# 1 / rms per column by a transpose on VectorE and two transfers of GpSimd's queue; squares and mean in one pass

## The chip, the core and the metric

The kernel runs on one core of a Trainium2 chip. The metric is the time of one execution in device microseconds; three executions of the kernel before took 994.14, 994.19 and 994.27 us, median 994.19. The engines are named as the profile names them: PE (TensorE; PEld is its weight load), DVE (VectorE), ACT (ScalarE), POOL (GpSimd) and SP (SyncE, which here only issues transfers).

## The reference

Two layers of a streaming encoder on 256 tokens of width 1024. Each layer has a half-step SwiGLU feed-forward part, a token mixer (latent attention with rotary keys in layer 0, forgetting attention in layer 1), a second half-step feed-forward part, and a gated embedding added to the residual; one norm ends the trunk. Each of these parts reads a normed residual:

```
def rms_norm(x, g):
    y = x * lax.rsqrt(jnp.mean(x * x, axis=-1, keepdims=True) + NORM_EPS)
    return y * g

def swiglu(x, w_in, w_out):
    gate, up = jnp.split(x @ w_in, 2, axis=-1)
    return (jax.nn.silu(gate) * up) @ w_out

for i in range(2):
    h = h + 0.5 * swiglu(rms_norm(h, ffn_norm[i, 0]), ffn_w_in[i, 0], ffn_w_out[i, 0])
    u = rms_norm(h, mix_norm[i])
    h = h + (mla_mixer if i == 0 else fox_mixer)(u, ...)
    h = h + 0.5 * swiglu(rms_norm(h, ffn_norm[i, 1]), ffn_w_in[i, 1], ffn_w_out[i, 1])
    h = h + jax.nn.sigmoid(rms_norm(h, ple_norm[i]) @ ple_w_gate[i]) * (p[i] @ ple_w_proj[i])
return rms_norm(h, final_norm)
```

## The kernel before

**Data.** The residual lies transposed as `hT`: 128 partitions by 8 blocks of the width, 256 tokens as columns. Activations and weights are f32, each split into a high part and the rest (`u`, `whi`, `wlo`), and a product is the sum of three products of the parts. A weight arrives as a 128x1024 tile `raw` (SP issues the transfer, four buffers); ACT copies its high part (`high`, L101), DVE subtracts it (`low`, L105), and seven pairs of parts can be alive. `W.pump()` adds one such step to the streams of ACT, DVE and SP; `W.get()` takes the next weight for PE.

**Order.** Nothing is reordered: each engine runs its instructions in the order in which the code adds them, and waits where an operand is not there yet.

**The norm.** `Norm` multiplies the residual by the gain and leaves 1 / rms for later: it is a factor of each token, so it can be applied to the product. While the residual's blocks come out, ACT squares them and POOL adds the squares up (`acc`, L303). `by_token` (L312) sums over partitions on PE (`pst`, L317), DVE makes the mean (`v`, L320) and POOL takes it to the power -1/2 (`rtok`, L322: 128 tokens on partitions, two columns). `by_column` (L324) turns that into a row of 256 columns on all partitions: PE multiplies `rtok`, repeated 128 times, by the identity (`pb`, L327), and ACT copies the product to `rb` (L330).

**The feed-forward part** (`ffn`, L334). The gate and up products of row block c go to two banks `pg` and `pu`; there are seven banks for all such products. The first pair (c = 0) is made by `blocks`, whose last steps wait for the residual's last blocks, then c = 1, and so on up to 21. `evacuate` multiplies a bank by `rb` on DVE (`two`, L341), POOL adds the two halves (`gu`, L343), ACT takes silu (`sg`), POOL multiplies (`hid`), and ACT and DVE split the product (`hs`). No bank is evacuated before `rb` is there. In the code before, `by_token` stands behind the gate block of c = 1 and `by_column` behind its up block.

**The other users.** `fox` uses `rb` in `project`, after its value products; there `by_token` comes at (c, k) = (0, 5) and `by_column` at (1, 0). `mla` and `ple` use it too. `by_column` stands in eight places of the run: the four feed-forward parts, twice in `mla`, once in `ple`, once in `fox`.

**The end** (`ple_by_token`, L865) works with tokens on partitions. `gated` applies the sigmoid, multiplies and adds to `h`, and lets ACT square `h` with a running sum (L885); `weigh` multiplies by the last gain (L888), `mean` adds a sum to the mean on DVE (L893), `root` takes the power on POOL (L906), `store` scales and sends the rows out. This runs over five pieces: 512 columns for each half of the tokens, then 512, 256 and 256.

Of the kernel before, what the change touches and what calls it, by code (L numbers as in the profile page):

```python
# [144 lines left out]
def trunk(ctx, tc, xT, xt, pT, pos, freq, bf, lead0, lead1, ffn_in, ffn_out, w_down, w_uq, w_ukv, mla_o,  # L145
# [7 lines left out]
    psum = ctx.enter_context(tc.tile_pool(name="psum", bufs=7, space=bass.MemoryType.PSUM))  # L153
    psm = ctx.enter_context(tc.tile_pool(name="psm", bufs=1, space=bass.MemoryType.PSUM))
# [55 lines left out]
    nc.gpsimd.memset(ones, 1.0)  # L210
    mhalf = const.tile([P, 2], F32, name="mhalf")
# [61 lines left out]
    class Norm:  # L273
# [38 lines left out]
        def by_token(self):  # L312
# [8 lines left out]
            self.rtok = work.tile([P, 2], F32, name="rtok", bufs=3)  # L321
            nc.gpsimd.tensor_tensor(self.rtok, v, mhalf, op=ALU.pow)  # L322

        def by_column(self):  # L324
            pb = psm.tile([P, T], F32, name="pb", tag="small")
            for t in range(2):
                nc.tensor.matmul(pb[:, t * P:(t + 1) * P], self.rtok[:, t:t + 1].to_broadcast([P, P]), ident,  # L327
                                 start=True, stop=True)
            self.rb = work.tile([P, T], F32, name="rb", bufs=3)
            nc.scalar.activation(self.rb, pb, AF.Copy)  # L330
            self.rb2 = self.rb.rearrange("p (o t) -> p o t", o=1).to_broadcast([P, 2, T])


    def ffn(norm, nxt, then=None, first=None, meanwhile=None, later=None):  # L334
# [38 lines left out]
        else:  # L373
            blocks(waits[0], norm.pair)
            W.pump(2)
        at = len(waits)
        for c in range(at, KF):
            pg = bank("pg")
            block(pg, norm.pair)
            if c == at:  # L380
                if not first:
# [6 lines left out]
            if c == at:  # L388
                norm.by_column()
# [309 lines left out]
    def fox(norm, nxt):  # L699
# [50 lines left out]
        for c in range(3):  # L750
            pv = [bank("pv0", (P, FV)), bank("pv1", (P, FV))]
            for k in range(KD):
# [6 lines left out]
                if (c, k) == (0, 5):  # L759
                    norm.by_token()  # L760
                elif (c, k) == (1, 0):
                    norm.by_column()
# [103 lines left out]
    def ple_by_token(pp, norm):  # L866
# [6 lines left out]
        sums = work.tile([P, 2, 3], F32, name="sums", bufs=1)  # L873
# [5 lines left out]
        def gated(t, ps, a, i):  # L879
# [5 lines left out]
            nc.scalar.activation(sg, h[:, t, a], AF.Square, accum_out=sums[:, t, i:i + 1])  # L885
# [3 lines left out]

        def mean(t, i):  # L890

            v = work.tile([P, 1], F32, name="v1", bufs=4)
            nc.vector.tensor_scalar(v, sums[:, t, i:i + 1], 1.0 / D, means[t], op0=ALU.mult, op1=ALU.add)  # L893
            means[t] = v
# [47 lines left out]
        for t in range(2):  # L942
            gated(t, ps[t], half[0], 0)
            weigh(t, half[0])
            mean(t, 0)
# [9 lines left out]
        gated(0, lasts[0], cuts[0], 1)  # L955
        weigh(0, cuts[0])
        mean(0, 1)
        root(0)
        gated(1, lasts[1], cuts[1], 1)
        store(0, [(nc.vector, a) for a in half])  # L960
        weigh(1, cuts[1])
        mean(1, 1)
        gated(1, lasts[2], cuts[2], 2)
        weigh(1, cuts[2])
        mean(1, 2)
# [176 lines left out]
    for i in range(2):  # L1142
# [98 lines left out]
```

## Time and profile before

| | |
|---|---|
| median of 3 executions | 994.19 us |
| the profiled execution | 994.27 us |
| its span, first to last instruction | 992.5 us |
| outside the span | 1.8 us |
| PE busy | 983.4 us, 99% of the span |
| DVE busy | 741.5 us, 75% |
| ACT busy | 515.3 us, 52% |
| POOL busy | 423.4 us, 43% |
| granted clock of PE, mean | 0.998 |

Busy time is that of an engine's instructions; overlapping ones are counted once. Matmuls are pipelined, so the time that one costs PE is the distance between the starts of its neighbours, not its own duration. An engine's idle time is put down to the event that ended it.

### The profile page before, as it was taken

The page shows a single profiled execution, that of the slowest core. Times are in us where ns is not written, and L with a number is a line of the kernel's source. Part 1 is how long each engine was busy: PE and PEld are TensorE (multiplying, and loading weights), DVE is VectorE, ACT ScalarE, POOL GpSimd, SP SyncE. Part 2 cuts the span into 40 slices and gives each one's busy share as a digit, 9 for nine tenths or more (in the row PEclk, how much of TensorE's full clock was granted, in tenths as well). Part 3 has the DMA queues.
Part 4 walks back from the last instruction along what each step waited for, and adds up shares of the span by engine and source line. Part 5 has one row for each costly group of instructions (what it writes and reads, how often), then busy time and mean ns, then how long its engine had stood idle before and what let it go on. Part 6 is the DMA issues. An engine that isn't in the chain of part 4 may idle for free.

```text
span 992.5 us, 15922 instructions
## 1 busy us (share of the span) xinstructions
PE 983.4 (99%) x5850; PEld 869.4 (88%) x5850; DVE 741.5 (75%) x1089; ACT 515.3 (52%) x820; POOL 423.4 (43%) x348
## 2 busy tenths in 40 slices
PE   9999999999999999999999999999999999999996
PEld 7888888998988888889988888899889888888885
DVE  6777879686878877667878786666877778786674
ACT  7555444466555544446655444446455555444552
POOL 0777730110277675111477773120211577761110
PEclk9999999999999999999999999999999999999999
DMA  8576666563456666665466666656543576666561
GB/s 324 184 249 209 198 180 192 175 194 105 148 172 207 182 188 175 205 203 168 149 210 203 186 184 180 193 179 217 149 149 106 177 209 196 187 179 204 179 210 43
DMA packets 53406, 182.26 MB, mean 184 GB/s; under 512 B 6225, under 2 KB 7761, under 8 KB 53201
## 3 DMA queue, kind: packets, MB, share of 16 engines
q1 hardware_dynamic: 52752, 180.40, 58.8%
q8 instruction: 46, 0.75, 0.3%
q10 hardware_dynamic: 576, 0.85, 0.3%
q14 instruction: 32, 0.25, 0.1%
HBM read 179.00 MB, written 1.05 MB: 181 GB/s over the span
## 4 chain that ended last, share of the span: by engine, by line
PE 98%; DMA 1%; issue 0%; ACT 0%; DVE 0%; SPq 0%; POOLq 0%; POOL 0%
PE po L247 16%; PE pu L247 16%; PE pg L247 16%; PE po L248 8%; PE pg L248 8%; PE pu L248 8%; PE ps L247 5%; PE ps L248 2%; PE ps L232 2%; PE ps L234 2%; PE ps L233 2%; PE pv L232 1%; PE pv L234 1%; PE pv L233 1%; PE po L476 1%; PE psc L794 1%
## 5 line engine op out<-in xcount | busy, mean ns | idle before, releaser
L105 DVE TENSOR_TENSOR wlo<-raw,whi 128x1024 fp32r<-128x1024 f32 (+2 forms) x339 | 417.0, 1239 | 13.2 <-ACT whi L101 12.6
L101 ACT ACTIVATE whi<-raw 128x1024 fp32r<-128x1024 f32 (+2 forms) x339 | 335.3, 1022 | 25.3 <-DMA raw<-in_ffn_in_dram 11.1
L343 POOL TENSOR_TENSOR gu<-two 128x256 f32<-128x256 f32 x176 | 234.7, 1334 | 122.5 <-DVE two L341 113.1
L247 PE MATMUL pg<-u,whi 128*128 128x512 f32 x702 | 251.1, 395 | 0.0
L247 PE MATMUL pu<-u,whi 128*128 128x512 f32 x702 | 250.9, 395 | 0.0
L247 PE MATMUL po<-hs,whi 128*128 128x512 f32 x704 | 246.8, 394 | 0.0
L248 PE MATMUL po<-hs,wlo 128*128 128x256 f32 x704 | 197.2, 280 | 0.0
L248 PE MATMUL pg<-u,wlo 128*128 128x256 f32 x702 | 197.0, 281 | 0.2 <-DVE wlo L228 0.2
L248 PE MATMUL pu<-u,wlo 128*128 128x256 f32 x702 | 196.8, 280 | 0.0
L247 PEld LDWEIGHTS po<-hs,whi 128*128 128x128 f32 x704 | 132.1, 188 | 31.3
L247 PEld LDWEIGHTS pg<-u,whi 128*128 128x128 f32 x702 | 131.8, 188 | 31.1 <-ACT whi L997 0.3
L247 PEld LDWEIGHTS pu<-u,whi 128*128 128x128 f32 x702 | 131.8, 188 | 30.9
L248 PEld LDWEIGHTS pg<-u,wlo 128*128 128x128 f32 x702 | 132.1, 188 | 0.7 <-DVE wlo L228 0.7
L248 PEld LDWEIGHTS po<-hs,wlo 128*128 128x128 f32 x704 | 132.3, 188 | 0.0
L248 PEld LDWEIGHTS pu<-u,wlo 128*128 128x128 f32 x702 | 132.0, 188 | 0.0
L303 POOL TENSOR_TENSOR acc<-acc,sq 128x256 f32<-128x256 f32 x42 | 46.2, 1101 | 174.2 <-ACT sq L298 152.7
L224 ACT ACTIVATE hs<-hid 128x256 fp32r<-128x256 f32 x88 | 36.8, 418 | 144.6 <-POOL hid L361 142.4
L361 POOL TENSOR_TENSOR hid<-sg,gu 128x256 f32<-128x256 f32 x88 | 106.3, 1208 | 6.9
L228 DVE TENSOR_TENSOR hs<-hid,hs 128x256 fp32r<-128x256 f32 x88 | 63.0, 716 | 49.7 <-ACT hs L224 49.7
L341 DVE TENSOR_TENSOR two<-pg,rb 128x512 f32<-128x512 f32 x88 | 60.3, 686 | 46.1 <-PE pg L248 38.6
L287 ACT ACTIVATE u<-state 128x256 fp32r<-128x256 f32 x47 | 24.0, 511 | 122.5 <-DVE state L408 104.3
L355 ACT ACTIVATE sg<-gu 128x256 f32<-128x256 f32 x88 | 36.8, 418 | 77.9 <-POOL gu L343 77.9
(258 smaller groups left out, 1162.2 us busy)
## 6 DMA issues: line engine op xcount, KB each, us to landing
raw<-in_ffn_in_dram SPq DMA_DIRECT2D x172, 512.0 KB, 4.0
raw<-in_ffn_out_dram SPq DMA_DIRECT2D x64, 512.0 KB, 3.6
raw<-in_ffn_out_dram SPq DMA_DIRECT2D x32, 384.0 KB, 3.4
raw<-in_fox_qk_dram SPq DMA_DIRECT2D x16, 512.0 KB, 4.5
raw<-in_mla_o_dram SPq DMA_DIRECT2D x8, 512.0 KB, 5.3
raw<-in_ple_gate_dram SPq DMA_DIRECT2D x8, 512.0 KB, 5.2
raw<-in_fox_o_dram SPq DMA_DIRECT2D x8, 512.0 KB, 3.5
raw<-in_ple_rows_dram SPq DMA_DIRECT2D x8, 512.0 KB, 4.6
```

What stands on the lines that cost most here:

```text
L101: self.nc.scalar.activation(self.pairs[i][0][:, c], self.raws[i][:, c], AF.Copy)
L105: self.nc.vector.tensor_sub(lo[:, c], self.raws[i][:, c], hi[:, c].bitcast(F32))
L224: nc.scalar.activation(hi, src, AF.Copy)
L228: nc.vector.tensor_sub(lo, src, hi.bitcast(F32))
L232: nc.tensor.matmul(ps, w[0], x[0], start=first, stop=False)
L247: nc.tensor.matmul(ps, hi, x[:, k], start=k == 0, stop=False)
L248: nc.tensor.matmul(ps[:, 1, :], lo, x[:, k, 0, :], start=False, stop=k == last)
L303: nc.gpsimd.tensor_add(new, self.acc, sq)
L341: nc.vector.tensor_mul(two, ps, norm.rb2)
L343: nc.gpsimd.tensor_add(gu[c, i], two[:, 0, :], two[:, 1, :])
L355: nc.scalar.activation(sg, gu.pop((c, 0)), AF.Silu)
L361: nc.gpsimd.tensor_mul(hid[c], gu.pop((c, 0)), gu.pop((c, 1)))
```

## The change

Three parts, told by what they do.

1. `spread` takes the place of `by_column` in three of the eight places: the second feed-forward part of layer 0, `fox`, and the second feed-forward part of layer 1. `by_token(soon=True)` writes `rtok` into columns 0 and 32 of a 128x64 tile `wide` that is zero elsewhere. DVE transposes `wide` in blocks of 32x32 (`turned`), so that the 256 factors lie in rows of 32 on four partitions. A transfer of POOL's queue writes them to a row of 256 in DRAM, and a second one reads that row back onto all 128 partitions, as `rb`. The other five places keep `by_column` (the first feed-forward part of layer 1 by `soon=False`).
2. In those two feed-forward parts `by_token` and `spread` stand ahead of the blocks of c = 1: one `W.pump()`, `by_token`, one `W.pump()`, `spread`. In `fox`, `by_token` stays at (0, 5) and `spread` stands at (0, 7).
3. In `ple_by_token` the squares and their mean are made by one DVE instruction (`tensor_tensor_reduce`, which starts its sum from the mean so far) instead of ACT's square and `mean`.

```diff
@@
+    dram = ctx.enter_context(tc.tile_pool(name="dram", bufs=1, space=bass.MemoryType.DRAM))
@@
+    wide = const.tile([P, 2 * 32], F32, name="wide")
+    nc.gpsimd.memset(wide, 0.0)
+    firsts = wide.rearrange("p (t j) -> p t j", t=2)[:, :, 0]
@@
-        def by_token(self):
+        def by_token(self, soon=False):
...
-            self.rtok = work.tile([P, 2], F32, name="rtok", bufs=3)
+            self.rtok = firsts if soon else work.tile([P, 2], F32, name="rtok", bufs=3)
             nc.gpsimd.tensor_tensor(self.rtok, v, mhalf, op=ALU.pow)
@@
+        def spread(self):
+
+            turned = work.tile([P, 2 * 32], F32, name="turned", bufs=1)
+            nc.vector.transpose(turned, wide)
+            row = dram.tile([1, T], F32, name="row", bufs=4)
+            nc.gpsimd.dma_start(row.rearrange("o (t q j) -> (o q) t j", t=2, q=4),
+                                turned.rearrange("(q r) (t j) -> q r t j", q=4, t=2)[:, 0])
+            self.rb = work.tile([P, T], F32, name="rb", bufs=3)
+            nc.gpsimd.dma_start(self.rb, row.to_broadcast([P, T]))
+            self.both()
@@
             blocks(waits[0], norm.pair)
-            W.pump(2)
+            W.pump()
+            if soon:
+                norm.by_token(soon=True)
+            W.pump()
+            if soon:
+                norm.spread()
@@
             if c == at:
-                if not first:
+                if not (first or soon):
                     norm.by_token()
                 W.pump()
@@
             if c == at:
-                norm.by_column()
+                if first or not soon:
+                    norm.by_column()
@@
                 if (c, k) == (0, 5):
-                    norm.by_token()
-                elif (c, k) == (1, 0):
-                    norm.by_column()
+                    norm.by_token(soon=True)
+                elif (c, k) == (0, 7):
+                    norm.spread()
@@
             nc.vector.tensor_add(h[:, t, a], h[:, t, a], sg)
-            nc.scalar.activation(sg, h[:, t, a], AF.Square, accum_out=sums[:, t, i:i + 1])
+
+            v = work.tile([P, 1], F32, name="v1", bufs=4)
+            nc.vector.tensor_tensor_reduce(sg, h[:, t, a], h[:, t, a], 1.0 / D, means[t], op0=ALU.mult, op1=ALU.add,
+                                           accum_out=v)
+            means[t] = v
@@
-            ffn(n0, n1, AF.Exp)
+            ffn(n0, n1, AF.Exp, soon=False)
```

How the instructions stand on DVE where the second feed-forward part of layer 0 begins, before (`state` is the residual, `u` its split parts, `wlo` the rest of a weight, `two` an evacuated bank):

```order
L292 SCALAR_TENSOR_TENSOR u<-state,u 128x256
L105 TENSOR_TENSOR wlo<-raw,whi 128x1024 x4
L320 TENSOR_SCALAR v<-pst 128x2
L105 TENSOR_TENSOR wlo<-raw,whi 128x1024
L341 TENSOR_TENSOR two<-pg,rb 128x512
L341 TENSOR_TENSOR two<-pu,rb 128x512
L341 TENSOR_TENSOR two<-pg,rb 128x512
L105 TENSOR_TENSOR wlo<-raw,whi 128x1024
```

And in the changed kernel, the same place (line numbers have moved):

```order
L297 SCALAR_TENSOR_TENSOR u<-state,u 128x256
L105 TENSOR_TENSOR wlo<-raw,whi 128x1024 x3
L325 TENSOR_SCALAR v<-pst 128x2
L105 TENSOR_TENSOR wlo<-raw,whi 128x1024
L341 STREAM_TRANSPOSE turned<-wide 128x64
L105 TENSOR_TENSOR wlo<-raw,whi 128x1024
L360 TENSOR_TENSOR two<-pg,rb 128x512
L360 TENSOR_TENSOR two<-pu,rb 128x512
L360 TENSOR_TENSOR two<-pg,rb 128x512
L105 TENSOR_TENSOR wlo<-raw,whi 128x1024
```

`v` stands one weight earlier, the transpose is new, and the same five weights stand ahead of the first `two`.

On POOL at the same place, before:

```order
L303 TENSOR_TENSOR acc<-acc,sq 128x256 x6
L322 TENSOR_TENSOR rtok<-v,mhalf 128x2
L343 TENSOR_TENSOR gu<-two 128x256 x2
L361 TENSOR_TENSOR hid<-sg,gu 128x256
L343 TENSOR_TENSOR gu<-two 128x256 x2
```

And changed:

```order
L308 TENSOR_TENSOR acc<-acc,sq 128x256 x6
L327 TENSOR_TENSOR wide<-v,mhalf 128x2
L343 DMA row<-turned 4x2x32
L346 DMA rb<-row 128x256
L362 TENSOR_TENSOR gu<-two 128x256 x2
L380 TENSOR_TENSOR hid<-sg,gu 128x256
```

The two transfers stand between the power and the first `gu`; the second waits in POOL's queue for the first to land.

On DVE at the very end of the program, for the last piece of 256 columns, before:

```order
L883 TENSOR_TENSOR sgr<-fin,sgr 128x256
L884 TENSOR_TENSOR fin<-fin,sgr 128x256
L888 TENSOR_TENSOR fin<-fin 128x256
L893 TENSOR_SCALAR v_10630<-sums,v_10622 128x1
L901 TENSOR_SCALAR fin<-fin,r 128x640
```

And changed (the two `ISA` rows are the reduction and the read of its sum):

```order
L907 TENSOR_TENSOR sgr<-fin,sgr 128x256
L908 TENSOR_TENSOR fin<-fin,sgr 128x256
L911 ISA sgr,v_10627<-fin,v_10616 128x256
L911 ISA v_10627 128x1
L916 TENSOR_TENSOR fin<-fin 128x256
L923 TENSOR_SCALAR fin<-fin,r 128x640
```

The mean is now complete ahead of `weigh` (L916) instead of behind it, and ACT has no square left.

## Rows read from the trace of the kernel before

**Rows 1.** The profile's page: the span, PE's busy time with the number of its instructions, and the chain of work that ended last, by engine.

```profile
span 992.5 us, 15922 instructions
PE 983.4 (99%) x5850; PEld 869.4 (88%) x5850; DVE 741.5 (75%) x1089; ACT 515.3 (52%) x820; POOL 423.4 (43%) x348
PE 98%; DMA 1%; issue 0%; ACT 0%; DVE 0%; SPq 0%; POOLq 0%; POOL 0%
```

**Rows 2.** All waits of PE for another engine: what waited, for what, us in total, times, longest.

```profile
PE cold L988 <- DVE warm L985: 1.1, 1, 1.1
PE pg L248 <- DVE wlo L228: 0.2, 1, 0.2
PE po L476 <- ACT ptS L471: 0.2, 1, 0.2
```

**Rows 3.** The timeline of PE at the second feed-forward part of layer 0: start in us from the span's start, duration, engine, line, operation, count. `pb` is the product of `by_column`.

```profile
272.29 0.39 PE L247 MATMUL pu<-u,whi 128*128 128x512 f32 x1
...
272.64 0.60 PE L327 MATMUL pb<-ident,rtok 128*128 128x128 f32 x4
...
273.43 0.40 PE L247 MATMUL pg<-u,whi 128*128 128x512 f32 x1
...
273.79 0.39 PE L247 MATMUL pg<-u,whi 128*128 128x512 f32 x1
```

**Rows 4.** The same view in `fox`.

```profile
671.05 0.32 PE L234 MATMUL pv<-wlo,u 128*128 128x344 f32 x1
671.21 0.61 PE L327 MATMUL pb<-ident,rtok 128*128 128x128 f32 x4
...
671.82 0.32 PE L233 MATMUL pv<-whi,u 128*128 128x344 f32 x1
671.97 0.32 PE L234 MATMUL pv<-wlo,u 128*128 128x344 f32 x1
```

**Rows 5.** The same view at the second feed-forward part of layer 1, the product before `pb` and the second one behind it.

```profile
779.94 0.39 PE L247 MATMUL pu<-u,whi 128*128 128x512 f32 x1
...
781.08 0.40 PE L247 MATMUL pg<-u,whi 128*128 128x512 f32 x1
```

**Rows 6.** The timeline of POOL: the last sum of squares and the power in the second feed-forward part of layer 0, then the power in that of layer 1. In brackets the idle time before and what ended it.

```profile
263.39 0.88 POOL L303 TENSOR_TENSOR acc<-acc,sq 128x256 f32<-128x256 f32 x1 [0.39 <-ACT sq L298]
270.15 0.70 POOL L322 TENSOR_TENSOR rtok<-v,mhalf 128x2 f32<-128x2 f32 x1 [5.88 <-DVE v L320]
...
777.84 1.74 POOL L322 TENSOR_TENSOR rtok<-v,mhalf 128x2 f32<-128x2 f32 x1 [5.88 <-DVE v L320]
```

**Rows 7.** The timeline of DVE in the second feed-forward part of layer 0: four weights, the mean, the fifth weight, the first evacuated bank, and the third weight behind that bank.

```profile
263.59 5.17 DVE L105 TENSOR_TENSOR wlo<-raw,whi 128x1024 fp32r<-128x1024 f32 x4
269.92 0.16 DVE L320 TENSOR_SCALAR v<-pst 128x2 f32<-128x2 f32 x1 [1.16 <-PE pst L317]
270.17 1.25 DVE L105 TENSOR_TENSOR wlo<-raw,whi 128x1024 fp32r<-128x1024 f32 x1
273.70 0.69 DVE L341 TENSOR_TENSOR two<-pg,rb 128x512 f32<-128x512 f32 x1 [2.27 <-ACT rb L330]
...
283.22 1.21 DVE L105 TENSOR_TENSOR wlo<-raw,whi 128x1024 fp32r<-128x1024 f32 x1
```

**Rows 8.** The same in that of layer 1: the fifth weight, the first bank, the third weight behind it.

```profile
777.79 1.23 DVE L105 TENSOR_TENSOR wlo<-raw,whi 128x1024 fp32r<-128x1024 f32 x1
781.42 0.69 DVE L341 TENSOR_TENSOR two<-pg,rb 128x512 f32<-128x512 f32 x1 [2.40 <-ACT rb L330]
...
790.95 1.21 DVE L105 TENSOR_TENSOR wlo<-raw,whi 128x1024 fp32r<-128x1024 f32 x1
```

**Rows 9.** The timeline of PE: the start of the gate block of c = 1 in layer 0's second feed-forward part; the first use of the third weight behind the first bank there (up block of c = 4); and the same use in layer 1.

```profile
266.58 0.40 PE L247 MATMUL pg<-u,whi 128*128 128x512 f32 x1
...
287.31 0.28 PE L248 MATMUL pu<-u,wlo 128*128 128x256 f32 x1
...
795.01 0.28 PE L248 MATMUL pu<-u,wlo 128*128 128x256 f32 x1
```

**Rows 10.** The view of transfers, by line: what is moved, by whose queue, how often, KB of one, median us from issue to landing. POOL's queue has none. The third is 0.5 KB issued between weights on SP's queue.

```profile
kqv<-yz SPq DMA_DIRECT2D x16, 64.0 KB, 4.4
p_sb<-in_pT_dram ACTq DMA_DIRECT2D x2, 256.0 KB, 2.5
...
fr<-in_freq_dram SPq DMA_DIRECT2D x1, 0.5 KB, 3.2
```

**Rows 11.** The timeline of DVE for the last piece, and the last power on POOL.

```profile
985.49 0.43 DVE L883 TENSOR_TENSOR sgr<-fin,sgr 128x256 f32<-128x256 f32 x1 [0.75 <-ACT sgr L882]
985.95 0.42 DVE L884 TENSOR_TENSOR fin<-fin,sgr 128x256 f32<-128x256 f32 x1
986.40 0.42 DVE L888 TENSOR_TENSOR fin<-fin 128x256 f32<-128x256 f32 x1
986.95 0.21 DVE L893 TENSOR_SCALAR v<-sums,v 128x1 f32<-128x1 f32 x1
...
987.24 0.55 POOL L906 TENSOR_TENSOR r<-v,mhalf 128x1 f32<-128x1 f32 x1 [4.22 <-DVE v L893]
```

**Rows 12.** Groups by line and form: the attention's reduction (the same operation as the new one, there with one operand in a product bank) and the read of its sum; busy us, mean ns of one, idle before.

```profile
L442 DVE CUSTOM_DVE_ANT_0 pr<-psc,cmask 128x256 f32<-128x256 f32 x16 | 6.7, 419 | 0.0
...
L442 DVE DVE_READ_ACCUMULATOR2_ANT m<- 128x1 f32 x32 | 2.7, 83 | 0.0
```

More of the change, by code (lines that the diff above doesn't have):

```diff
@@ L330, in by_column, with both, ffn @@
             nc.scalar.activation(self.rb, pb, AF.Copy)
+            self.both()
[7 more added lines that the diff above has]
+            nc.gpsimd.dma_start(self.rb, row.to_broadcast([P, T]))
+            self.both()
+        def both(self):
             self.rb2 = self.rb.rearrange("p (o t) -> p o t", o=1).to_broadcast([P, 2, T])
-    def ffn(norm, nxt, then=None, first=None, meanwhile=None, later=None):
+    def ffn(norm, nxt, then=None, first=None, meanwhile=None, later=None, soon=True):
         hs = big.tile([P, KF, 2, T], F32R, name="hs", tag="big")
@@ L872, in ple_by_token, with gated @@
         half = [slice(0, N), slice(N, D)]
-        sums = work.tile([P, 2, 3], F32, name="sums", bufs=1)
         def rows(ps, w, x, k, a, t, last):
             mm3(ps, [x[:, k, i, t * P:(t + 1) * P] for i in range(2)], [i[:, a] for i in w[1:]], k == 0, k == last)
-        def gated(t, ps, a, i):
+        def gated(t, ps, a):
             sg = work.tile([P, N], F32, name="sgr", tag="pair2", bufs=4)[:, :a.stop - a.start]
@@ L884, in gated @@
             nc.vector.tensor_add(h[:, t, a], h[:, t, a], sg)
-            nc.scalar.activation(sg, h[:, t, a], AF.Square, accum_out=sums[:, t, i:i + 1])
+            v = work.tile([P, 1], F32, name="v1", bufs=4)
+            nc.vector.tensor_tensor_reduce(sg, h[:, t, a], h[:, t, a], 1.0 / D, means[t], op0=ALU.mult, op1=ALU.add,
+                                           accum_out=v)
+            means[t] = v
         def weigh(t, a):
             nc.vector.tensor_mul(es[:, t, a], h[:, t, a], gain[:, a])
[L890 to L894, printed above, removed]
         def store(t, cuts):
@@ L942, in ple_by_token @@
         for t in range(2):
-            gated(t, ps[t], half[0], 0)
+            gated(t, ps[t], half[0])
             weigh(t, half[0])
-            mean(t, 0)
         cuts = [(0, N, D), (1, N, N + T), (1, N + T, D)]
@@ L954, in ple_by_token @@
         cuts = [slice(a, b) for t, a, b in cuts]
-        gated(0, lasts[0], cuts[0], 1)
+        gated(0, lasts[0], cuts[0])
         weigh(0, cuts[0])
-        mean(0, 1)
         root(0)
-        gated(1, lasts[1], cuts[1], 1)
+        gated(1, lasts[1], cuts[1])
         store(0, [(nc.vector, a) for a in half])
         weigh(1, cuts[1])
-        mean(1, 1)
-        gated(1, lasts[2], cuts[2], 2)
+        gated(1, lasts[2], cuts[2])
         weigh(1, cuts[2])
-        mean(1, 2)
         root(1)
```

## The prediction

> **What bounds the kernel now.** I read the page first: PE is busy for 983.4 of 992.5 us, and the chain that ended last is PE for 98% [rows 1]. Then all waits of PE for another engine: 0.4 us after the start-up [rows 2]. So the run is the sum of PE's instructions, plus a few us at either end. An instruction taken from PE's stream shortens the run by what it cost there, as long as no other engine becomes late by it; everything taken from or given to DVE, ACT or POOL counts for nothing until PE has to wait. Third I read the timelines of the places where `by_column` goes, on PE [rows 3 to 5], POOL [rows 6] and DVE [rows 7, 8], to see how late `rb` may come. Last the end, where PE is done and the other engines alone set the time [rows 11].
>
> **PE's share.** Three products `pb` go. In layer 0 two products in a row start 1.14 us apart with `pb` between them (272.29 and 273.43), where their step is 0.36 [rows 3]: cost 1.14 - 2 x 0.36 = 0.42. In `fox` it is 671.05 to 671.82 with a step of 0.15 [rows 4]: 0.77 - 0.30 = 0.47. In layer 1 it is 1.14 again [rows 5]: 0.42. The sum is 1.31 us. `pst` is only moved, and the sum it reads is done at 263.39 + 0.88 = 264.27 [rows 6], while its new place on PE comes up at 266.58 [rows 9]: 2.3 us of reserve, no wait. The three copies of ACT that go lie beside PE's work and are worth nothing.
>
> **How late `rb` may come.** Behind the first bank, DVE, POOL and ACT work as one chain (bank, `gu`, `sg`, `hid`, `hs`, next banks, weights), so if the first bank moves, the weights behind it move as much. PE has five more weights in hand, as the order shows the same five ahead of the first bank in both kernels. The tightest of the later ones is the third behind the first bank. In layer 0 it ends at 283.22 + 1.21 = 284.43 [rows 7], and PE first uses it at 287.31 [rows 9]: 2.88 us; PE will be there 0.42 earlier, which leaves 2.46. The first bank stood at 273.70 [rows 7], so `rb` may come until 276.2. In layer 1: 795.01 - (790.95 + 1.21) - 0.42 = 2.43, and 781.42 + 2.43 = 783.85 [rows 8, 9]. Free product banks are a weaker bound, since seven of them carry PE well past that moment.
>
> **When `rb` does come.** Layer 0: of the four weights, at 5.17 / 4 = 1.29 each, `v` now waits for three: 263.59 + 3.88 = 267.47, and ends 0.16 later [rows 7]. The fourth weight follows at once, to about 268.9. The power on POOL has two durations. Started 0.02 us ahead of a weight on DVE it took 0.70; started 0.05 us behind one it took 1.74 and ended 0.56 behind that weight's end (779.58 against 779.02) [rows 6 to 8]. In the new order the weight is ready and starts first, so I take the second form: 268.9 + 0.56 = 269.4. The transpose of 64 columns has no row; `v` with 2 columns takes 0.16 and 256 columns take 0.42 [rows 7, 11], so 0.2, and `turned` is there at 269.6. Layer 1 runs the same sequence 507.7 us later (781.42 against 273.70): 777.3. What is left for the two transfers, one after the other, is 6.6 and 6.5 us: 3.3 us each.
>
> The Trainium skill, "DMA: Bandwidth & Descriptors", section "Anatomy of one DMA — SWDGE (gpsimd) path", puts a transfer of GpSimd's queue at about 2.0 us plus its bytes, most of it the receipt of the write. By an estimate from that page `rb` would be there at about 273.6; the trace has no transfer of that queue to compare.
>
> No transfer of POOL's queue is in the trace, so I bound one by the nearest rows: 2.5 us for 256 KB on ACT's queue, which like POOL's is not the weights' own; 3.2 us for 0.5 KB that stood among weights; 4.4 us for transfers behind others in one queue [rows 10]. Two take 5.0 to 8.8 us. I take 2.5 each, the row with a queue of its own: `rb` at 274.6 and 782.3, 0.9 later than before and 1.6 ahead of need. What POOL itself needs to issue a transfer has to fit into that 1.6. POOL has nothing queued behind the transfers but `gu`, which needs `rb` anyway. DVE holds its stream at the first `two`, with weights behind it, and this is the reserve worked out above. The fifth weight, behind the transpose, is not held up: in before it started only at 270.17 [rows 7], after the transpose's 269.6. The cost of the wait in the two feed-forward parts is 0. In `fox`, `rb` is first used when the value products are done, many us behind the spread: 0.
>
> **The end.** Before, the last addition ends at 986.37, and the last power starts at 987.24 and ends at 987.79 [rows 11], behind ACT's square and `mean`. Now the reduction takes 0.42 and its read 0.08 [rows 12], with starts a little closer than that: the mean is there at about 986.9. If POOL starts at once, the power ends at 986.9 + 0.55 plus a signal, 987.5: a gain of 0.3. But `weigh` on DVE (0.42) starts right behind the read, and by the two forms of the power above POOL then ends 0.56 behind it: 987.9, a loss of 0.1. The earlier pieces give DVE some 0.9 us more to do (reductions and reads for two `mean`s), against 0.75 us of idle time before the last piece [rows 11]: up to 0.1 of loss. Between -0.3 and +0.2 I take 0, nearer to the second form, since DVE's own next instruction needs no signal.
>
> The rule behind both places is in the Trainium skill, "SBUF — State Buffer", section "SBUF: two separate sides": a DVE instruction with two SBUF inputs and a GpSimd one that reads SBUF share a port pair, and whichever starts first keeps it for its whole instruction. The trace agrees (0.70 against 1.74 us). Without that rule the end would be 0.3 us shorter.
>
> **The sum.** The profiled execution took 994.27 us, 0.08 over the median: 994.27 - 1.31 + 0 = 992.96, against the median 992.9. Its own range is 992.5 to 993.3 (the end's bounds, and 0.1 of reading error).
>
> **The rivals.**
> 1. *The transfers are slow, and PE waits (slower than before).* At 4.4 us each, `rb` comes at 269.6 + 8.8 = 278.4 and 786.1, 2.2 us late in each part, and PE waits for a weight: 992.9 + 4.4 = 997.3. For it: the 4.4 us row, and the weights' refill runs in the same stretch. Against: that row's transfers queue behind their own kind, and here each waits for the one before it only. It begins to cost at 3.3 us each, eats the gain at 3.6, and is over 0.2% at 4.1.
> 2. *DVE's weight holds up the first transfer.* If POOL can issue nothing while the fifth weight runs, as its power could not, the transfer starts at 270.17 + 1.25 = 271.4 and 779.0 [rows 7, 8]: `rb` at 276.4 and 784.0, 0.2 late in each: 993.3; with 3.0 us per transfer instead of 2.5, 1.2 late in each: 995.3. Against: the transfer is issued at 269.6, half a us ahead of that weight. The Trainium skill, "SBUF — State Buffer", in the same section, speaks for this one: GpSimd cannot write the descriptors of its own transfers while DVE holds the shared ports. No run here shows it.
> 3. *The gain is hidden*: a stage that other work paces gives the 1.31 us back later, and the time stays at 994.2. Against: PE waited 0.4 us in all [rows 2].
> 4. *The end gains more*: the power is free at once and the last piece comes earlier, 992.6.
>
> **How the numbers follow.** Forecast 0.52 (992.5 to 993.3); rival 1 0.17, of which 0.11 above 996.2; rival 2 0.16, of which 0.02 above 996.2; rival 3 0.07; rival 4 0.08, of which 0.04 below 992.2 (it would take something more that I do not see). 0.2% is 2.0 us, about what a measurement of this kernel can tell from no change: 992.2 to 996.2. So faster 0.04, the same 0.83, slower 0.13. The range 992.4 to 995.4 leaves out about 0.14 of rival 1, 0.03 of rival 2 and 0.04 below; with rival 1's cases there it holds 8 in 10.
>
> **What would show it.** Right: `pb` on PE falls from 32 to 20 records; PE's steps at the three places close up to 0.36 and 0.15; the first `two` starts before 276.2 - and, counted from PE's block of c = 1 (266.58 in before), within 9.6 us; PE's waits stay under 0.5 us in all. Wrong: a wait of PE for `wlo` in the up block of c = 4 or near it (rival 1 or 2, told apart by when the first transfer's landing stands against the fifth weight); a span shorter by less than 1 us without a wait of PE (rival 3); a start-up or an end outside the span that has grown by POOL's queue.

## The result and the profile after

The kernel after took 996.36 us (median of 15 executions, 995.62 to 997.12), the kernel before beside it 994.34 us (993.85 to 994.93): ratio 1.002, 95% interval 1.0013 to 1.0027. It is slower by 2.0 us, where 1.3 us less were forecast. The profiled execution took 996.22 us, its span is 994.5, and PE's mean granted clock is the same 0.998.

The page of the kernel after, the lines that answer to [rows 1]:

```profile
span 994.5 us, 15916 instructions
PE 983.5 (99%) x5838; PEld 868.8 (87%) x5838; DVE 739.5 (74%) x1097; ACT 511.7 (51%) x807; POOL 428.1 (43%) x355
PE 90%; DVE 4%; DMA 2%; POOL 2%; issue 1%; ACT 1%; POOLq 0%; DVEq 0%; ACTq 0%
```

PE has 12 instructions less, the `pb` of three places, but the chain of work that ended last is no longer PE alone: DVE, DMA and POOL have 8% of it. PE's waits say where (columns as in [rows 2]):

```profile
PE pg L253 <- DVE wlo L105: 2.1, 2, 1.1
PE cold L1006 <- DVE warm L1003: 1.1, 1, 1.1
PE pu L253 <- DVE wlo L105: 0.5, 2, 0.2
PE po L501 <- ACT ptS L496: 0.2, 1, 0.2
```

The first and the third line are new: two waits in each of the two feed-forward parts, for a weight of DVE. The timeline of PE in layer 0 has them in the gate and the up block of c = 4, that is at the second and the third weight behind the first bank (start, duration, in brackets the wait). The rows of PEld below them are the weight loads of the same two products, and of one more in the up block of c = 3, at the first weight behind the bank, where the product itself has no bracket:

```profile
285.33 0.38 PE L253 MATMUL pg<-u,wlo 128*128 128x256 f32 x1 [1.08 <-DVE wlo L105]
...
288.64 0.39 PE L253 MATMUL pu<-u,wlo 128*128 128x256 f32 x1 [0.24 <-DVE wlo L105]
...
281.20 0.19 PEld L253 LDWEIGHTS pu<-u,wlo 128*128 128x128 f32 x1 [0.25 <-DVE wlo L105]
...
285.33 0.19 PEld L253 LDWEIGHTS pg<-u,wlo 128*128 128x128 f32 x1 [1.41 <-DVE wlo L105]
...
288.64 0.19 PEld L253 LDWEIGHTS pu<-u,wlo 128*128 128x128 f32 x1 [0.56 <-DVE wlo L105]
```

Why DVE was late with them stands in its own timeline and in POOL's, first layer 0 and then layer 1 (they answer to [rows 6 to 8]):

```profile
267.59 1.61 POOL L327 TENSOR_TENSOR wide<-v,mhalf 128x2 f32<-128x2 f32 x1 [3.51 <-DVE v L325]
269.24 0.24 DVE L341 STREAM_TRANSPOSE turned<-wide 128x64 f32<-128x64 f32 x1 [0.59 <-POOL wide L327]
269.80 0.75 POOL L343 DMA_DIRECT2D row<-turned  x1 [0.59 <-DVE turned L341]
269.92 1.23 DVE L105 TENSOR_TENSOR wlo<-raw,whi 128x1024 fp32r<-128x1024 f32 x1 [0.43 <-ACT whi L101]
274.64 0.59 POOL L346 DMA_DIRECT2D rb<-row  x1 [4.09 <-DMA row<-turned]
277.85 0.69 DVE L360 TENSOR_TENSOR two<-pg,rb 128x512 f32<-128x512 f32 x1 [6.71 <-DMA rb<-row]
...
778.80 0.62 POOL L343 DMA_DIRECT2D row<-turned  x1 [0.57 <-DVE turned L341]
783.39 0.58 POOL L346 DMA_DIRECT2D rb<-row  x1 [3.97 <-DMA row<-turned]
786.61 0.69 DVE L360 TENSOR_TENSOR two<-pg,rb 128x512 f32<-128x512 f32 x1 [6.35 <-DMA rb<-row]
```

Up to the transpose all is on time: `turned` is there at 269.5, forecast 269.6. Then `row` takes 4.84 us from its issue to the issue of `rb` (269.80 to 274.64; 4.59 in layer 1), and `rb` another 3.2 until DVE can start. Together 8.05 and 7.8 us, where 2.5 + 2.5 were taken. DVE stands still for 6.7 us with all its later weights behind the first `two`.

**Where the 2.0 us come from.** Put side by side product by product, PE's starts in both traces differ by these steps, in us: at the start-up (the first 9 us) -0.19; where `pb` stood -0.44 in layer 0, -0.44 in `fox`, -0.45 in layer 1; `pst` +0.45 at its new place and -0.45 at its old one, in both feed-forward parts; at the waits +0.20 in c = 3 and +1.87 in c = 4 of layer 0 (1.36 + 0.51), and +1.80 in c = 4 of layer 1 (1.30 + 0.50); small ones +0.11. The last product starts 2.46 later:

```profile
987.07 0.28 PE L239 MATMUL ps<-wlo,u 128*128 128x256 f32 x1
```

(984.60 in the kernel before). The span has grown by 2.0 only, so the end behind that product has become 0.5 shorter. The gains of the change are there, 1.33 us on PE and, of the 0.5 at the end, 0.2 that belong to the new end (below, under "The end"); the waits in the two parts cost 3.87.

### The profile page after: what moved, and what is told of

Its sections match the earlier page's. It is cut to its first block, busy times and chain, and to the rows that moved or that the text cites. A ratio compares the mean times of both kernels' runs of the same rounds, so it can differ in the third digit from the quotient of the medians.

```text
span 994.5 us, 15916 instructions
## 1 busy us (share of the span) xinstructions
PE 983.5 (99%) x5838; PEld 868.8 (87%) x5838; DVE 739.5 (74%) x1097; ACT 511.7 (51%) x807; POOL 428.1 (43%) x355
## 3 DMA queue, kind: packets, MB, share of 16 engines
HBM read 179.39 MB, written 1.05 MB: 181 GB/s over the span
## 4 chain that ended last, share of the span: by engine, by line
PE 90%; DVE 4%; DMA 2%; POOL 2%; issue 1%; ACT 1%; POOLq 0%; DVEq 0%; ACTq 0%
PE po L252 16%; PE pu L252 15%; PE pg L252 15%; PE po L253 8%; PE pu L253 8%; PE pg L253 7%; PE ps L252 4%; PE ps L253 2%; PE ps L237 2%; PE ps L239 2%; PE ps L238 2%; DVE wlo L105 1%; DVE state L542 1%; DMA row<-turned 1%; PE pv L237 1%
## 5 line engine op out<-in xcount | busy, mean ns | idle before, releaser
L105 DVE TENSOR_TENSOR wlo<-raw,whi 128x1024 fp32r<-128x1024 f32 (+2 forms) x339 | 417.0, 1239 | 13.8 <-ACT whi L101 13.5
L362 POOL TENSOR_TENSOR gu<-two 128x256 f32<-128x256 f32 x176 | 227.8, 1295 | 118.1 <-DVE two L360 108.7
L380 POOL TENSOR_TENSOR hid<-sg,gu 128x256 f32<-128x256 f32 x88 | 113.4, 1288 | 6.9
L233 DVE TENSOR_TENSOR hs<-hid,hs 128x256 fp32r<-128x256 f32 x88 | 59.2, 673 | 58.4 <-ACT hs L229 58.4
```

The source lines that it names most:

```text
L105: self.nc.vector.tensor_sub(lo[:, c], self.raws[i][:, c], hi[:, c].bitcast(F32))
L233: nc.vector.tensor_sub(lo, src, hi.bitcast(F32))
L362: nc.gpsimd.tensor_add(gu[c, i], two[:, 0, :], two[:, 1, :])
L380: nc.gpsimd.tensor_mul(hid[c], gu.pop((c, 0)), gu.pop((c, 1)))
```

## The experiments

**Which part costs.** Two kernels with one part each: `spread` in `fox` alone, with `by_column` in both feed-forward parts and the old end; and the new end alone, in the kernel before. The diff shows the first as an edit of the kernel after, cut to its main lines: the old end goes back whole, with ACT's squares and `mean`. The second is the third part of the change put into the kernel before.

```diff
-    def ffn(..., later=None, soon=True):
+    def ffn(..., later=None, soon=False):
...
-            gated(0, lasts[0], cuts[0])
+            gated(0, lasts[0], cuts[0], 1)
+            mean(0, 1)
```

> Left as before: the end and both feed-forward parts; only `fox` has its `spread`. Theory A (the loss comes from the late `rb` of the two feed-forward parts alone): one `pb` of PE goes and nothing waits, since `rb` is not used until the value products are done: 0.4 us faster than the kernel before, 993.9, with no new wait of PE over 0.2 us. Theory B (the use of GpSimd's queue, or the start-up with `wide`, costs something by itself, wherever it stands): as slow as the kernel after or part of the way there, 994.8 to 996.4.

> Only the end is changed (squares and their mean in one pass of DVE). Theory A: the end gains 0.2 to 0.4 us, as the trace of the kernel after has it between the last product and the last output: 993.9 to 994.1, the same within what can be measured. Theory B (the longer DVE stream at the end costs, as the prediction's upper bound has it): 0.1 to 0.2 us slower, 994.4 to 994.5, the last power on POOL starting later behind the last addition than before.

Measured: `fox` alone 993.68 us, ratio 0.9992 (0.9983 to 1.0001), and PE's only waits are the small ones of [rows 2]; the new end alone 993.99, ratio 0.9994 (0.9985 to 1.0003). Neither differs from the kernel before by more than the interval, and both medians lie on the side of a gain, as theory A has it. Neither part alone brings the loss, so GpSimd's queue is not dear by its mere use; the feed-forward parts are what is left.

**What the late `rb` does.** One weight more on DVE ahead of the first bank, in the idle time before it:

```diff
                 if first or not soon:
                     norm.by_column()
+                if soon and not first:
+                    W.pump()
                 for x, ps in enumerate(waits):
                     gate(x, ps[0], x)
```

> The kernel after with one weight more made by DVE ahead of the first bank in the two feed-forward parts, in the time in which DVE waits for `rb`. Theory A (PE waits only since the weights stand behind the first bank in DVE's stream): `rb` comes as late as in the kernel after (first `two` at 277.8 +- 0.4 and 786.6 +- 0.4), PE does not wait in the blocks of c = 4, and the 3.7 us go: 992.7 (992.4 to 993.2), faster than before by 1.5. Theory B (the late bank holds up the whole chain of bank, `gu`, `hid` and product banks, and the weight is only its first sign): the wait moves to a later block or to a product bank, and at least 1.5 us of the 3.7 stay: 994.2 to 996.4.

Measured: 992.77 us, ratio 0.9984 (0.9975 to 0.9992). The waits for `wlo` L105 are gone:

```profile
PE po L503 <- ACT ptS L498: 0.2, 1, 0.2
PE pg L253 <- DVE wlo L233: 0.2, 1, 0.2
```

with the start-up's own left out here (one weight load waits 0.4 us in the first feed-forward part of layer 1, which the change leaves alone, and PE's starts step back by 0.3 there), and in DVE's timeline `rb` is as late as ever:

```profile
272.28 1.23 DVE L105 TENSOR_TENSOR wlo<-raw,whi 128x1024 fp32r<-128x1024 f32 x1 [0.58 <-ACT whi L101]
278.61 0.69 DVE L360 TENSOR_TENSOR two<-pg,rb 128x512 f32<-128x512 f32 x1 [5.10 <-DMA rb<-row]
...
785.98 0.69 DVE L360 TENSOR_TENSOR two<-pg,rb 128x512 f32<-128x512 f32 x1 [4.99 <-DMA rb<-row]
```

The first row is the weight that is new there; the two others are the first banks (278.61 lies 0.4 past the expected window, in a run whose start-up was 0.45 longer than that of the kernel after; 785.98 lies 0.2 ahead of its window, in a run in which PE is 1.4 earlier there). So theory A holds: a late `rb` costs PE nothing but the weights that stand behind it, and one weight in front of it is worth 3.6 us. Product banks, `gu` and `hid` have the reserve that the prediction gave them.

**Why the transfers are slow: the queue.** The same transfers issued by ACT on its own queue, instead of by POOL:

```diff
-            nc.gpsimd.dma_start(row.rearrange(...), turned.rearrange(...)[:, 0])
+            nc.scalar.dma_start(row.rearrange(...), turned.rearrange(...)[:, 0])
...
-            nc.gpsimd.dma_start(self.rb, row.to_broadcast([P, T]))
+            nc.scalar.dma_start(self.rb, row.to_broadcast([P, T]))
```

> The kernel after with the six transfers issued by ACT on its own queue instead of POOL on GpSimd's. Theory L (GpSimd's queue is slow by itself: descriptors that POOL writes, and DVE's fifth weight in the way of that): row `p_sb` of ACT's queue took 2.5 us, so `rb` comes at about 274.9 in layer 0 and 783.6 or less in layer 1, PE does not wait over 0.4 us in all, 992.7. Theory T (the transfers are slow because the refill of the weights fills the DMA engines, whoever issues them): `row` takes 3.7 us or more from issue to landing here too, `rb` comes after 277, PE waits 1 us or more in each part, 995.5 to 996.5. Between the two: each transfer 3 to 3.6 us, 993 to 995.

Measured: 996.74 us, ratio 1.0021 (1.0012 to 1.003). ACT's queue in layer 0, and what it held up in `fox`:

```profile
269.54 1.11 ACTq L343 DMA_DIRECT2D row<-turned  x1
273.85 0.33 ACTq L346 DMA_DIRECT2D rb<-row  x1
...
676.69 0.32 PE L740 MATMUL pz<-ident,zt 128*96 128x128 f32 x1 [1.03 <-ACT zt L801]
```

`row` takes 4.31 us from issue to issue (4.11 in layer 1), against 4.84 and 4.59 on POOL's queue; the first `two` starts at 276.91 and 786.15, which is 3.06 and 2.88 behind the issue of `rb`. So neither theory had it whole. Against the kernel after the queue is worth 0.5 us for `row` and 0.2 to 0.3 for `rb`; the runs with `row` on POOL's queue in these two places have 4.36 to 5.02 us for it, so the gap is a small one. PE's loss in the feed-forward parts falls from 3.87 to 1.8 us; but most of `row`'s time stays. The total did not fall, because ACT waits in its own stream until `row` has landed, and in `fox` its evacuations stand behind that wait: PE loses 1.7 us there, a step of +1.20 at the row above and +0.54 at the next `pz`.

**Why the transfers are slow: DVE's weight, or the traffic.** First DVE's weight. Behind the issue of `row` DVE starts its fifth weight; here it is moved behind the first `two`, and the refill goes on:

```diff
-                W.pump()
+                if first or not soon:
+                    W.pump()
...
-                    gate(x, ps[0], x)
+                    gate(x, ps[0], x if first or not soon else 1)
```

> The kernel after with DVE's fifth weight moved behind the first `two` in the two feed-forward parts, so that DVE does nothing while `row` is issued and moved; the weights' refill on the DMA engines goes on. Read is the time from the issue of `row` to that of `rb` on POOL: 4.84 us in layer 0 and 4.59 in layer 1 in the kernel after. Theory L (DVE's weight keeps POOL from writing the descriptors): 3.3 to 3.6 us. Theory T (the refill of the weights) and theory I (this transfer takes that long by itself): 4.2 us or more. The whole kernel is slower than the kernel after by any theory, since PE then waits for the fifth weight: 997 to 1000.

POOL in this run, layer 0 and layer 1:

```profile
270.04 0.75 POOL L343 DMA_DIRECT2D row<-turned  x1 [0.59 <-DVE turned L341]
275.01 0.59 POOL L346 DMA_DIRECT2D rb<-row  x1 [4.22 <-DMA row<-turned]
...
780.12 0.62 POOL L343 DMA_DIRECT2D row<-turned  x1 [0.57 <-DVE turned L341]
784.48 0.58 POOL L346 DMA_DIRECT2D rb<-row  x1 [3.74 <-DMA row<-turned]
```

DVE in layer 0, idle from the transpose to the first bank:

```profile
278.24 0.69 DVE L360 TENSOR_TENSOR two<-pg,rb 128x512 f32<-128x512 f32 x1 [8.51 <-DMA rb<-row]
```

4.97 and 4.36 us with DVE idle: theory L falls. (The run, one execution, took 998.39 us; PE's waits for `wlo` L105 add up to 4.2 us, one of 1.3 for the weight that was held.)

Then the transfers by themselves. Near the end no weight is left to load. Two pairs more were put there, which nothing uses: one on POOL's queue with DVE idle, then the same with three subtractions on DVE, then with loads of old weights on SP's queue beside it; the second pair goes on SP's queue each time.

```diff
         ws = W.get(KD // 2)
+        norm.spread()
         for t in range(2):
             gated(t, ps[t], half[0])
             weigh(t, half[0])
+        norm.spread(nc.sync)
```

The subtractions stand behind the first `spread`, the loads ahead of it:

```diff
+        for i in ws[:3]:
+            x = W.pool.tile([P, D], F32, name="raw", bufs=W.RAW)
+            nc.vector.tensor_sub(x, i[1].bitcast(F32), i[2].bitcast(F32))
```

```diff
+        for src in W.plan[-4:]:
+            nc.sync.dma_start(W.pool.tile([P, D], F32, name="raw", bufs=W.RAW), src)
```

> The kernel after with two more pairs of the transfers `row` and `rb` near the end, where no weight is left to load and the DMA engines stand still: one pair on GpSimd's queue while DVE waits for ACT, one on SP's queue a few us later; nothing uses what they bring. Read is the time from the issue of `row` to that of `rb`. Theory T: without the refill of the weights `row` takes as long as `rb` does in the kernel after, 3.2 us or less from issue to issue, on both queues. Theory I: 4.0 to 4.4 us on GpSimd's queue, as in `fox` (4.20). Theory L: 3.3 to 3.6 here. On SP's queue theory I has about 0.3 to 0.5 us less than on GpSimd's, as the run on ACT's queue had. The time of the kernel: within 1 us of 996.4.

> As the run before it, and DVE does three more subtractions of the weights' form (128x1024, about 1.2 us each, of data already there) right behind the transpose, while POOL issues the pair. Theory L: the first packet of `row` comes 0.7 to 3 us later behind its issue than with DVE idle, and the time from the issue of `row` to that of `rb` grows as much. Theories T and I: as with DVE idle, within 0.3 us. The time of the kernel: 996 to 997.5.

> The run with DVE idle near the end once more (two extra pairs of transfers that nothing uses), and now SP loads the last four weights, 512 KB each, a second time into buffers that nothing reads, just when POOL issues its pair. In the quiet stretch POOL's `row` took 1.97 us from issue to the issue of `rb`. Theory T (a small transfer stands behind the loads of the weights on the DMA engines): 4 to 5 us again, with the first packet 2.5 us or more behind the issue, as in the feed-forward parts. Rival (it is not the traffic but something else that differs there, PE's or ACT's work or the state of the queue): 2.0 to 2.5 us.

POOL with DVE idle and no traffic, and the pair on SP's queue:

```profile
972.30 0.62 POOL L343 DMA_DIRECT2D row<-turned  x1 [9.26 <-DVE turned L341]
974.27 0.58 POOL L346 DMA_DIRECT2D rb<-row  x1 [1.35 <-DMA row<-turned]
...
981.67 0.61 SPq L343 DMA_DIRECT2D row<-turned  x1
983.42 0.33 SPq L346 DMA_DIRECT2D rb<-row  x1
```

With three subtractions of DVE right behind the transpose, DVE's row and POOL's two:

```profile
972.41 3.45 DVE L967 TENSOR_TENSOR raw<-whi,wlo 128x1024 f32<-128x1024 f32 x3
972.78 0.62 POOL L343 DMA_DIRECT2D row<-turned  x1 [9.42 <-DVE turned L341]
974.75 0.58 POOL L346 DMA_DIRECT2D rb<-row  x1 [1.35 <-DMA row<-turned]
```

With four weights loaded once more, SP's row and POOL's two:

```profile
967.74 4.47 SPq L964 DMA_DIRECT2D raw<-in_ple_rows_dram  x4
972.94 0.62 POOL L343 DMA_DIRECT2D row<-turned  x1 [9.57 <-DVE turned L341]
977.41 0.58 POOL L346 DMA_DIRECT2D rb<-row  x1 [3.84 <-DMA row<-turned]
```

The DMA engines in the same 2 us, first without and then with the loads. The columns are the stretch, its length, busy us (and number of instructions) of PE, PEld, DVE, ACT and POOL, PE's granted clock, the mean busy share of the DMA engines, and GB/s:

```profile
972.00:974.00 2.00, 2.00 (x10) 1.61 (x10) 0.00 (x0) 0.00 (x0) 0.62 (x1) 1.00 0.01 1
...
972.00:974.00 2.00, 2.00 (x10) 1.63 (x9) 0.65 (x2) 0.00 (x0) 0.62 (x1) 1.00 0.94 289
```

The wait of POOL in the brackets is the reading: 1.35 us, 1.35 us, 3.84 us. From issue to issue `row` takes 1.97 us alone, 1.97 beside three weights' worth of DVE, 1.75 on SP's queue, and 4.47 beside the loads. Without the traffic `row` is 2.2 to 2.9 us shorter than in the three places of the kernel after (4.20 us in `fox`), and traffic added brings 2.5 us back; DVE does nothing to it. Theory T holds for `row`, and L and I fall.

The traces also hold the transfers' packets and landings, and these say where the time goes (us behind the issue of the transfer, all on POOL's queue):

| | first packet | last packet's end | landing |
|---|---|---|---|
| `row`, quiet | 1.19 | 1.36 | 1.68 |
| `row`, beside three subtractions | 1.20 | 1.35 | 1.68 |
| `row`, beside four loads | 2.27 | 3.65 | 4.18 |
| `row`, kernel after, layer 0 | 2.70 | 4.02 | 4.55 |
| `rb`, quiet | 1.29 | 2.88 | 3.21 |
| `rb`, kernel after, layer 0 | 1.30 | 2.87 | 3.19 |

Of the 2.5 us that the loads add to `row`, 1.1 lie ahead of its first packet, 1.2 between the first and the last, and 0.2 behind the last. (The first packet beside the loads comes 2.27 us behind the issue, a little less than the 2.5 that theory T expected.) `rb` is a different matter: it takes 3.2 us on POOL's queue in the quiet stretch as in the feed-forward parts, where by then the refill has run dry, and 2.9 on SP's queue. So the traffic explains `row`; `rb` takes longer than 2.5 us without any. The stretches of the kernel after show both (columns as above):

```profile
268.00:270.00 2.00, 2.00 (x14) 1.74 (x13) 0.97 (x3) 1.06 (x1) 1.41 (x2) 1.00 1.04 285
270.00:272.00 2.00, 2.00 (x14) 1.73 (x13) 1.15 (x1) 1.12 (x2) 0.55 (x1) 1.00 0.89 326
272.00:274.00 2.00, 2.00 (x13) 1.77 (x12) 0.00 (x0) 1.22 (x1) 0.00 (x0) 1.00 1.02 380
274.00:276.00 2.00, 2.00 (x14) 1.74 (x13) 0.00 (x0) 0.00 (x0) 0.59 (x1) 1.00 0.23 86
```

`row` is issued and moved at a DMA share of 0.89 to 1.04, `rb` at 0.23. The three runs, one execution each, took 996.61, 996.94 and 997.24 us.

**Is the wait as long as `rb` is late?** `pst` earlier on PE (by 1.4 us in the traces, not the 1.7 expected), and `v`, the power and the transpose one weight earlier on DVE:

```diff
     def blocks(ps, x, within=None):
...
                 part(p, w, x, ks, KD - 1)
+            if within and ks.start == 0:
+                within()
...
-            blocks(waits[0], norm.pair)
-            W.pump()
-            if soon:
-                norm.by_token(soon=True)
+            blocks(waits[0], norm.pair, soon and (lambda: norm.by_token(soon=True)))
             W.pump()
             if soon:
                 norm.spread()
+            W.pump()
```

> The kernel after with `pst` placed 1.7 us earlier on PE (between the products of the first two blocks) and `v`, the power and the transpose one weight earlier on DVE in both feed-forward parts; still five weights in hand ahead of the first bank. Theory A (PE waits as much as `rb` is late): `row` is issued about 1.1 us earlier, the transfers take what they take in the kernel after, 7.6 to 8 us in all, the first `two` starts at about 276.2 to 276.7 in layer 0 and 785 to 785.5 in layer 1, and the wait of PE in a part falls from 1.8 to between 0.1 and 0.7: 992.8 to 994.0. Theory L adds that the weight behind the transpose, held up by its copy on ACT, no longer stands in the way: the first `two` 1.3 us earlier still, no wait, 992.7. Rival: the wait is set by something else than `rb`, and the time stays at 996.

Measured: 994.22 us, ratio 0.9995 (0.9986 to 1.0004); the profiled span is 993.0. The first `two` starts at 277.41 and 785.11, and the waits in the blocks of c = 4 are short ones, the first in layer 0

```profile
284.90 0.38 PE L253 MATMUL pg<-u,wlo 128*128 128x256 f32 x1 [0.24 <-DVE wlo L105]
```

`rb` came somewhat later than the window for layer 0 (this run's start-up was 0.6 longer than that of the kernel after), and the time lies 0.2 above the expected range. Six parts from three runs can be held against the deadline of the prediction (276.2 and 783.85, moved by what PE had gained or lost up to there): late by 1.9 and 1.6 us in the kernel after, 0.85 and 0.75 here, 0.9 and 0.55 on ACT's queue. PE's starts behind the waits, against those ahead of them, are 2.0 and 1.8, 1.0 and 0.9, 1.05 and 0.7 later. The loss is the lateness and 0.15 to 0.2 more, in all six. With one weight more ahead of the bank `rb` is late by 2.2 and 2.4 by the same count, and PE loses nothing there.

**The gains without the wait.** The change without its feed-forward part, beside the kernel with one weight more:

> The change without its feed-forward part: `spread` in `fox` and the new end, `by_column` in both feed-forward parts. Theory A: the two gains add, 0.7 from the one and 0.35 from the other by the medians of the single runs, 0.4 and 0.4 by the trace: 993.2 to 993.7, faster than before by 0.6 to 1.1, and slower than the kernel with one weight more by 0.5 to 0.9 (its two `pb`). Rival: the gains don't add, 993.8 or more.

> The kernel with one weight more ahead of the first bank once more, beside the run without the feed-forward part on the same chip: 992.4 to 993.1 and faster than that one if the two `pb` of the feed-forward parts are a gain (0.42 us each); the same as that one or slower if a late `rb` costs something that PE's waits do not show.

Measured beside each other: 993.46 us, ratio 0.9990 (0.9981 to 0.9999), and 992.68 us, ratio 0.9984 (0.9975 to 0.9992). The second repeats the 992.77 of the first time. The gains of `fox` and the end come to 0.9 together, of 0.7 + 0.35. The second kernel's median is 0.8 us lower, about 2 x 0.42, but the two ratios' intervals overlap, and the traces do not give all of the 0.8 to the two `pb`. PE's last product starts at 984.07 in the one and 983.25 in the other; 0.4 of that stands already behind the start-up, which differs from run to run. Behind it the second kernel has the two steps of -0.44 and about -0.4 that the first lacks, and a step of +0.3 in the first feed-forward part of layer 1, where a weight load waits for DVE, as in the earlier run of the same kernel. Net the second is 0.4 ahead by the traces, and whether it is faster than the first is not settled.

## Why the prediction was wrong

- **PE's share** (three `pb` for 1.31 us): right in kind and in size. The three places gave 0.44, 0.44 and 0.45 us, 1.33 in all (the products named as two in a row have one between them, and the sum rightly takes two steps off). `pst`, counted as free to move, cost 0.45 at its new place and gave back 0.45 at its old one.
- **The deadline of `rb`** (276.2 and 783.85, from the third weight behind the first bank): right to 0.2 us, as the six parts above show. The wait begins earlier, with 0.2 us at the first weight in layer 0 and most of it at the second (1.36 us in layer 0, 1.30 in layer 1), and the third adds the rest.
- **`turned` at 269.6, the power in its long form**: right. The power took 1.61 us behind the start of a weight, the transpose 0.24, and `turned` was there at 269.5.
- **The step that failed: 2.5 us per transfer.** "I take 2.5 each, the row with a queue of its own." `row` took 4.84 and 4.59 us and `rb` 3.2 each; the two together took 8.05 and 7.8 us instead of 5.0, against a reserve of 6.6 and 6.5. For `row` it did not matter much whose queue it is, but what the DMA engines do meanwhile. Windows of the kernel before, first around the two transfers `p_sb` that gave the 2.5 us, then where `row` was to go (columns as above):

```profile
402.00:404.50 2.50, 2.50 (x16) 2.19 (x15) 2.50 (x3) 2.48 (x4) 0.85 (x1) 1.00 0.49 129
909.60:912.20 2.60, 2.60 (x17) 2.29 (x16) 2.57 (x3) 2.58 (x4) 0.90 (x1) 1.00 0.45 131
...
270.00:272.00 2.00, 2.00 (x13) 1.73 (x13) 1.33 (x2) 1.05 (x2) 0.70 (x1) 1.00 0.85 320
272.00:274.00 2.00, 2.00 (x14) 1.80 (x14) 0.30 (x1) 0.85 (x3) 0.00 (x0) 1.00 0.98 322
```

  DMA share 0.45 to 0.49 there, their own 256 KB included, against 0.85 to 0.98 here. The trace of before held this warning, though not the price: the 0.5 KB row `fr` took its 3.2 us at a share of 0.74, and two of these are 6.4, just inside the reserve. The other bound, 2 x 4.4 = 8.8, was the nearer one. `rb` was too low by 0.7 us for another reason: it takes 3.2 us in the quiet stretch too. By an estimate from the quiet run the two would have come to 1.97 + 3.2 = 5.2 us without the traffic, within the reserve; so it is the traffic around `row` that turned the gain into a loss.
- **Rival 1** (slow transfers, 997.3, chance 0.17) is what happened: PE waits for a weight, above all in the blocks of c = 4. Its reason for was right ("the weights' refill runs in the same stretch"), its reason against was not: that `row` waits for no transfer of its own kind does not keep it clear of the weights. Its price was 4.4 us; measured 3.87, since the two transfers took 0.75 to 1.0 us less than 8.8.
- **Rival 2** (DVE's weight holds up the transfer) would also have given a late `rb`, and its first sign was there: in layer 0 of the kernel after the first packet of `row` moved at 272.5, 1.3 us after the weight had ended. It falls by two runs: `row` took 4.97 and 4.36 us with no weight behind the issue, and 1.97 with three. The lock of the page that it named is told there of DVE in a two-port mode, or with two SBUF inputs against a GpSimd operation that reads SBUF (the Trainium skill, "SBUF — State Buffer", section "SBUF: two separate sides"); the prediction stretched that to the writing of descriptors beside a plain subtraction, which no run here shows.
- **Rivals 3 and 4** (the gain hidden; the end gains more): the third falls, since the steps of all three `pb` are there in the kernel after and in the version with one weight more; of the fourth a part is there, 0.2 us at the end, below.
- **The estimate from the page on transfers** (about 2.0 us plus bytes): the Trainium skill, "DMA: Bandwidth & Descriptors", section "Anatomy of one DMA — SWDGE (gpsimd) path", agrees roughly with `row` in the quiet stretch (1.68 us to the landing, 1.97 to the next issue) and not with `rb`, 3.2 us there, where the page's bytes would add 0.3 to the 2.0 (an estimate from that page). Nor does its division show here: it has most of the 2.0 us in the receipt of the write, and in the quiet stretch 0.32 us lie between the end of `row`'s last packet and its landing, and 1.19 ahead of the first. The same page has in "Latency and other measured facts" that the DRAM's latency is 0.2 us on average and 2 us under high load, and that the fixed cost is smaller when the load is lighter; the 4.47 us beside the loads go that way. By the packets it is not the receipt behind the last one that grew most (0.32 to 0.53 us), but the time ahead of and between them; what keeps the packets waiting, no run here separates.
- **The end** (-0.3 to +0.2, taken as 0): in its range, a gain of 0.2. The last addition ends at 988.77 and the last power at 990.05, 1.28 us; before it was 1.42 (986.37 to 987.79) [rows 11]. The rows of the kernel after:

```profile
988.81 0.48 DVE L911 CUSTOM_DVE_ANT_0 sgr<-fin,v 128x256 f32<-128x256 f32 x1
...
989.22 0.42 DVE L916 TENSOR_TENSOR fin<-fin 128x256 f32<-128x256 f32 x1
...
989.38 0.67 POOL L928 TENSOR_TENSOR r<-v,mhalf 128x1 f32<-128x1 f32 x1 [3.73 <-DVE v L911]
```

  The power is lengthened by DVE's `weigh` (0.67 against 0.55), but it ends 0.41 us behind it and not 0.56 as in the second form; the reduction took 0.48 instead of 0.42. Counted from the start of PE's last product the power ends 0.20 earlier, at 2.99 us instead of 3.19, in the kernel after as in the run with the new end alone; `fox` alone has 3.19. All behind the last product is 0.50 us shorter (7.38 instead of 7.88). The other 0.3 lies behind the power, where the rows are scaled and sent out, and it is not the new end's: this stretch takes 4.70 us in the kernel before and 4.69 with the new end alone, and 4.40 in the kernel after and in `fox` alone with the old end. Over all runs it takes 4.28 to 4.70; what sets it was not tried.
- **The range** held the forecast and small delays. The rows that come nearest to the stretch's traffic (`fr` at a DMA share of 0.74, the 64 KB transfers at 0.73) give 6.4 and 8.8 us for two, against a reserve of 6.6 and 6.5; set beside the share, the case with a wait deserved more than 0.17.

## What to carry to other kernels

Before taking a transfer's price from another row, compare the DMA share of the two stretches: 1 KB took 1.97 us where the engines stood still and 4.1 to 5.0 us where weights were loaded, on POOL's queue and on ACT's. Where the stretch is busier than that of any row, the row's price may be too low (here 3.2 us to the landing at a share of 0.74, and 4.55 at 0.89 to 1.04). A wait on an in-order engine is paid by what is queued behind it; before moving the wait, put the work that others need in front of it: one weight more ahead of the bank turned 2.0 us of loss into 1.6 us of gain (1.7 in the second run). And a transfer issued by an engine with work of its own moves the wait into that engine's stream (ACT in `fox`).

## What the runs showed of the hardware

- A transfer of 1 KB to DRAM took 1.97 us (POOL) and 1.75 us (SP) from issue to the next issue in a quiet stretch, and 4.47 us beside four loads of 512 KB; reading the row back to 128 partitions (128 KB) took 2.9 us on SP's queue in the quiet stretch, and 3.2 on POOL's there and in the feed-forward parts of the kernel after.
- Of the 2.5 us that the loads added to that 1 KB, 0.2 lay between the last packet and the landing, and 2.3 ahead of and between the packets.
- Three subtractions of DVE with both inputs in SBUF, 3.45 us in a row across the whole of POOL's issue, did not lengthen a transfer of POOL's queue (1.35 us of waiting with and without), while the power on POOL beside one such subtraction takes 1.61 to 1.74 us instead of 0.70 [rows 6].
- A wait of PE is read from the weight load: the matmuls' brackets give 1.08 and 0.24 us, and PE's later products came 1.36 and 0.51 us later; the weight loads (PEld) of the same products have 1.41 and 0.56. A wait of 0.25 on a weight load put them back by 0.20, with no bracket on the matmul.
